# More weight buffers, low-half products last, deferred transposes and a moved modulation in a hybrid attention and FFN layer

## The chip, the core and the metric

The kernel runs on one core of a Trainium2 chip. TensorE (PE in the profile) multiplies, VectorE (DVE) and ScalarE (ACT) work elementwise, GpSimd (POOL) does a few additions and starts small transfers, and SyncE (SP) starts nearly all loads. The metric is the device time of one execution in microseconds (us); lower is better.

## The reference

One layer of a diffusion backbone over 256 latent tokens and 256 context tokens of width 2048, in float32. The parts that matter here:

```python
mod_x = split(silu(c) @ w_mod + b_mod, 6)         # shift1, scale1, gate1, shift2, scale2, gate2
h = rms_norm(x, g_mix) * (1 + scale1) + shift1    # the context with its own shift and scale
q, k, v, qb, kb, vb, rb, lr, ga, gb = split(h @ w_in)
o_attn = windowed_attention(rope(norm(q)), rope(norm(k)), v, context keys, sink)
o_gla = gated linear attention in two directions, started from the context
y = sigmoid(ga) * (o_attn @ w_attn_o) + sigmoid(gb) * ((norm(o_gla) * silu(rb)) @ w_gla_o)
x = x + gate1 * (y @ w_out)
u = conv3(modulate(x, g_ffn, shift2, scale2) @ w_up)   # 2 x 5632 columns
x = x + gate2 * ((silu(u_a) * u_g) @ w_down)
```

Every weight matrix is read from memory once; there are about 400 MB of them.

## The kernel before

**Exact products from halves.** PE multiplies float32 numbers that are cut into a high half `hi` and a low half `lo = x - hi`, and a product is the sum of three: high by high, high by low, low by high. `wsplit` (line 143) loads a half chunk of weights, two blocks of 128 rows by 512 columns, 512 KB, into a raw buffer, and cuts it: ACT copies it to `whi` (line 61), DVE subtracts to `wlo` (line 62). There are four raw buffers (`wr`, line 38) and three pairs of half buffers (`wh`, line 39).

**Two kinds of projection.** `proj_nat` (line 152) makes tokens by features: for each half chunk and each tile of 128 tokens, the activations are the stationary operand and the weights stream in 512 columns; lines 163 to 165 are the three products. `proj_T` (line 169) makes features by tokens: the weights are stationary and 256 tokens stream; lines 186, 188 and 189 are the three. Sums collect in four PSUM banks (`acc`); a projection with two token tiles takes two, one over latent and context tokens takes four. After its last half chunk, `evac` takes the banks out.

**Work beside the projections.** `tick` (line 124) runs once ahead of each half chunk. It advances a generator in `beside` (the linear attention `gla_A`, or the windowed attention `attend`) at a pace, and takes steps of a list `bg_steps` at the rate `bg_rate`. That list holds the later modulation: `mod_latent` (line 225) reads `w_mod` in 512 KB steps through the same raw buffers, and DVE multiplies each by a column of silu(c) and adds up in `macc` (line 239, two operations a step). After eight steps DVE transposes and reduces, and PE sums across partitions in the small product `pcl` (line 247). Parts 3, 4, 2 and 5 (shift2, scale2, gate1, gate2) are four times eight steps each.

**Stages in order.** Start: x and the context are transposed, shift1 and scale1 are made on PE, and with each group of rows of h that part of QB (two projections), KB and VB is added up (`add_to`, line 363). Then linear attention per head beside the next head's KB or VB block; the keys KA and values VA; four query blocks QA and one GA block with the windowed attention beside them; four RB blocks; the merge, which for each quarter of the columns runs GA, the attention's output matrix, GB and the linear attention's output matrix; the output projection; and the FFN, whose up projection is cut in a half of six blocks and one of five, each followed by its part of the down projection.

**Transposes at the end of a projection.** Token-major results that are needed feature-major are transposed on PE inside `evac`: `ptk` (line 680) and `ptq` (line 696) behind `norm_rope`, `to_T` (line 777, tile `pto`) in the RB blocks and the merge, and `ptx` (line 846) in the output projection. `rows_from_cols` (line 257) spreads a gate over all partitions: a transpose on PE, a copy, and two transfers by POOL by way of memory. gate1 is made ahead of the output projection, gate2 ahead of the up projection.

**What orders the instructions.** The program's order gives each instruction a rank, and a planner with its own idea of durations lays out each engine's stream ahead of the run: at each point the engine takes the highest ranked instruction that the planner takes to be ready. The split in `wsplit` has a raised rank. On the chip each engine works off its stream in order and waits where an input is late.

## Time and profile before

| | |
|---|---|
| median of three runs (us) | 2060.81 (2058.01 to 2062.3) |
| span of the profiled execution (us) | 2061.8 |
| mean granted PE clock | 0.990 |
| read from memory | 409.63 MB, 200 GB/s over the span |
| PE, DVE, ACT busy | 97%, 68%, 45% |

The profiled execution is told of by its span alone; it lies 1.0 us above the median of the runs. A row of groups reads: line, engine, operation, tile written <- tiles read, shapes, count | busy us, mean ns | idle time before and what ended it. A row of waits reads: who waited <- for whom: total us, times, longest. "SPq" is the queue of loads. Busy matmuls overlap, since a product starts before the one ahead of it has ended; the pace of PE is read from the distance of starts.

### The profile page before, as it was taken

To read this page: it belongs to the slowest core of one execution; us is meant where nothing else is said; L and a number is where in the kernel's file an instruction comes from. 1 tells how busy PE (TensorE), PEld (TensorE's weight loads), DVE (VectorE), ACT (ScalarE), POOL (GpSimd) and SP (SyncE) were. 2 spreads that over 40 slices of the span, in tenths; PEclk is the share of its full clock that TensorE was granted. 3 is DMA by queue.
4 is the path that set the end of the run, shared out by engine and by line. 5 is a ranking of instruction groups with operands and counts; after the bars stand their busy time and mean duration, and the time that the engine had idled before them with its cause. 6 is when DMAs were issued, how large, how long until landed. Compare 5 with 4: busy or idle time off the path is not lost.

```text
span 2061.8 us, 30115 instructions
## 1 busy us (share of the span) xinstructions
PE 1999.2 (97%) x11792; PEld 1721.8 (84%) x11792; DVE 1405.7 (68%) x2149; ACT 937.4 (45%) x1306; POOL 41.9 (2%) x62
## 2 busy tenths in 40 slices
PE   6899999999999999999999999899999999999999
PEld 4679888888787777777787788899999889999987
DVE  4666778978867888777767665666666555666654
ACT  3323464552346665443334344554455334445533
POOL 0001100001000000000000000000000000000000
PEclk8999999999999999999999999999999999999999
DMA  9976434347664466787888875566666566666664
GB/s 347 337 247 197 120 111 123 113 118 226 213 186 114 121 194 192 254 270 260 264 279 272 294 235 184 164 184 184 184 183 184 194 193 187 184 184 183 183 209 150
DMA packets 214350, 413.71 MB, mean 201 GB/s; under 512 B 12548, under 2 KB 21092, under 8 KB 213184
## 3 DMA queue, kind: packets, MB, share of 16 engines
q1 hardware_dynamic: 212320, 406.89, 63.3%
q0 software_dynamic: 1360, 4.74, 0.8%
q8 instruction: 92, 1.51, 0.3%
q14 instruction: 50, 0.41, 0.1%
q10 hardware_dynamic: 528, 0.17, 0.0%
HBM read 409.63 MB, written 2.11 MB: 200 GB/s over the span
## 4 chain that ended last, share of the span: by engine, by line
PE 60%; issue 18%; DMA 11%; DVE 8%; ACT 2%; POOL 0%; DVEq 0%; ACTq 0%; POOLq 0%
PE acc L189 10%; PE acc L186 10%; PE acc L188 10%; PE acc L165 8%; PE acc L164 8%; PE acc L163 8%; DMA raw<-in_w_mod 8%; DVE wlo L62 3%; DVE macc L239 2%; DMA raw<-in_w_in 2%; PE pm L210 1%; PE pa L503 1%; ACT whi L61 1%; DMA raw<-in_w_gla_o 1%; PE po L589 1%
## 5 line engine op out<-in xcount | busy, mean ns | idle before, releaser
L61 ACT ACTIVATE whi<-raw 128x1024 fp32r<-128x1024 f32 x568 | 601.4, 1059 | 863.7 <-PE acc L165 366.4
L62 DVE TENSOR_TENSOR wlo<-raw,whi 128x1024 fp32r<-128x1024 f32 x568 | 693.3, 1222 | 428.3 <-ACT whi L61 422.7
L186 PE MATMUL acc<-h2h,whi 128*128 128x256 f32 x1408 | 399.5, 284 | 1.3 <-ACT h2h L346 1.3
L188 PE MATMUL acc<-h2l,whi 128*128 128x256 f32 x1408 | 399.5, 284 | 0.0
L189 PE MATMUL acc<-h2h,wlo 128*128 128x256 f32 x1408 | 399.2, 284 | 0.0
L186 PEld LDWEIGHTS acc<-h2h,whi 128*128 128x128 f32 x1408 | 271.3, 193 | 1.9 <-ACT h2h L346 1.8
L188 PEld LDWEIGHTS acc<-h2l,whi 128*128 128x128 f32 x1408 | 271.3, 193 | 0.2
L189 PEld LDWEIGHTS acc<-h2h,wlo 128*128 128x128 f32 x1408 | 271.3, 193 | 0.0
L239 DVE SCALAR_TENSOR_TENSOR macc<-raw,ccol,macc 128x512 f32<-128x512 f32 x240 | 180.6, 752 | 100.5 <-DMA raw<-in_w_mod 97.2
L163 PE MATMUL acc<-whi,h01hi 128*128 128x512 f32 x352 | 139.5, 396 | 0.9 <-ACT whi L61 0.9
L164 PE MATMUL acc<-wlo,h01hi 128*128 128x512 f32 x352 | 139.1, 395 | 1.3 <-DVE wlo L62 1.2
L163 PE MATMUL acc<-whi,h00hi 128*128 128x512 f32 x352 | 139.2, 395 | 0.0
L164 PE MATMUL acc<-wlo,h00hi 128*128 128x512 f32 x352 | 139.0, 395 | 0.2 <-DVE wlo L62 0.2
L165 PE MATMUL acc<-whi,h00lo 128*128 128x512 f32 x352 | 138.6, 394 | 0.0
L165 PE MATMUL acc<-whi,h01lo 128*128 128x512 f32 x352 | 138.2, 392 | 0.0
L163 PE MATMUL acc<-whi,ah 128*128 128x512 f32 x352 | 137.0, 389 | 0.0
L164 PE MATMUL acc<-wlo,ah 128*128 128x512 f32 x352 | 137.0, 389 | 0.0
L165 PE MATMUL acc<-whi,al 128*128 128x512 f32 x352 | 136.9, 389 | 0.0
L164 PEld LDWEIGHTS acc<-wlo,h01hi 128*128 128x128 f32 x352 | 66.4, 189 | 16.0 <-DVE wlo L62 3.2
L163 PEld LDWEIGHTS acc<-whi,h01hi 128*128 128x128 f32 x352 | 66.4, 189 | 14.3 <-ACT whi L61 1.3
L164 PEld LDWEIGHTS acc<-wlo,h00hi 128*128 128x128 f32 x352 | 66.2, 188 | 14.1 <-DVE wlo L62 1.3
L165 PEld LDWEIGHTS acc<-whi,al 128*128 128x128 f32 x352 | 66.1, 188 | 13.8
(369 smaller groups left out, 3393.2 us busy)
## 6 DMA issues: line engine op xcount, KB each, us to landing
raw<-in_w_in SPq DMA_DIRECT2D x208, 512.0 KB, 4.2
raw<-in_w_up SPq DMA_DIRECT2D x176, 512.0 KB, 3.7
raw<-in_w_mod SPq DMA_DIRECT2D x128, 512.0 KB, 3.9
raw<-in_w_down SPq DMA_DIRECT2D x88, 512.0 KB, 3.8
mraw<-in_w_mod SPq DMA_DIRECT2D x32, 1024.0 KB, 10.2
raw<-in_w_attn_o SPq DMA_DIRECT2D x32, 512.0 KB, 4.8
raw<-in_w_gla_o SPq DMA_DIRECT2D x32, 512.0 KB, 5.2
raw<-in_w_out SPq DMA_DIRECT2D x32, 512.0 KB, 3.8
```

Source lines behind the costliest of these rows:

```text
L61: S.activation(hi, src, AF.Copy)
L62: V.tensor_tensor(lo, src, hi.bitcast(F32), op=ALU.subtract)
L163: PE.matmul(banks[i], ahi, hi[:, k, :], start=(kt == kts[0]), stop=False)
L164: PE.matmul(banks[i], ahi, lo[:, k, :], start=False, stop=False)
L165: PE.matmul(banks[i], alo, hi[:, k, :], start=False, stop=(kt == kts[-1]))
L186: PE.matmul(o, whi, ahi, start=(kt == kts[0] and b == 0), stop=False, skip_group_check=True)
L188: PE.matmul(o, whi, alo, start=False, stop=False, skip_group_check=True)
L189: PE.matmul(o, wlo, ahi, start=False, stop=(kt == kts[-1]), skip_group_check=True)
L210: PE.matmul(a[0][q:q + 32, :], cS[:, kt, :], raw[:, k, :], start=(kt < 4), stop=(kt >= 12))
L239: V.scalar_tensor_tensor(a[0], raw[:, k, :], ccol[:, kt:kt + 1], a[0], op0=ALU.mult, op1=ALU.add)
L503: PE.matmul(pa[:, t, :], k2[:, dt, t * P:(t + 1) * P], q2[:, dt, tq * P:(tq + 1) * P], start=(dt == 0), stop=(dt == 1))
L589: PE.matmul(po, x_, y_[:, s, :], start=(n == 0), stop=(n == 11))
```

## The change

- The raw buffers go from four to five, the pairs of half buffers from three to four. Room for them comes from the descriptor space of GpSimd's transfers (`dynamic_dma_scratch_size=4096`); the parameter rows of `columns` move to another pool.
- In both kinds of projection the products with the weights' low half are issued after all products with the high half of that half chunk.
- `defer(n, fn)` puts a piece of an evacuation on a list; `tick` counts down and runs it ahead of the half chunk that comes n + 1 ticks later. The transposes of KA, QA, RB, the merge and the output projection go there, and the last product of `mod_latent`. `flush` runs what is left.
- The steps of part 5 (gate2) leave the list that runs up to the merge and run beside the first half of the up projection, at 0.36 a half chunk; gate2 is spread over the partitions after it. The rates of the other steps change: 0.7 to 0.3, 2.0 to 1.6, 0.5 to 0.52.
- The windowed attention runs at 1.4 steps a half chunk instead of 0.8, starting at -2.9, so from the third half chunk on.

Removed comments aside, the diff is:

```diff
--- before.py
+++ after.py
@@ -35,8 +35,8 @@
...
     big = pool(name="big", bufs=16)
-    wr = pool(name="wr", bufs=4)
-    wh = pool(name="wh", bufs=3)
+    wr = pool(name="wr", bufs=5)
+    wh = pool(name="wh", bufs=4)
     f2 = pool(name="f2", bufs=1)
...
@@ -100,7 +100,7 @@
...
     def columns(name, parts, eng=G):
-        rows = W2("mod", "rows", [P, P])
+        rows = sm.tile([P, P], F32, name="rows", tag="t128", bufs=2)
         n = 0
...
@@ -115,14 +115,27 @@
...
     beside = []
+    later = []
+    def defer(n, fn):
+        later.append([n, fn])
+    def flush():
+        while later:
+            later.pop(0)[1]()
...
+        for e in later:
+            e[0] -= 1
+        while later and later[0][0] < 0:
+            later.pop(0)[1]()
         if beside:
...
@@ -161,13 +174,16 @@
...
                     PE.matmul(banks[i], ahi, hi[:, k, :], start=(kt == kts[0]), stop=False)
-                    PE.matmul(banks[i], ahi, lo[:, k, :], start=False, stop=False)
-                    PE.matmul(banks[i], alo, hi[:, k, :], start=False, stop=(kt == kts[-1]))
+                    PE.matmul(banks[i], alo, hi[:, k, :], start=False, stop=False)
+            for i, l in enumerate(lhs):
+                for k in range(nk):
+                    kt = k0 + k
+                    PE.matmul(banks[i], l(kt)[0], lo[:, k, :], start=False, stop=(kt == kts[-1]))
         for i in range(len(lhs)):
...
@@ -175,26 +191,27 @@
...
             hi, lo = wsplit(w[k0 * P:(k0 + nk) * P, c0:c0 + 512])
-            for f in range(4):
-                for k in range(nk):
-                    kt = k0 + k
-                    whi, wlo = (x[:, k, f * P:(f + 1) * P] for x in (hi, lo))
-                    for i, r in enumerate(rhs):
-                        b = (f % per) if n == 1 else i
-                        o = banks[f // per][:, b * T:(b + 1) * T]
-                        ahi, alo = r(kt)
-                        PE.matmul(o, whi, ahi, start=(kt == kts[0] and b == 0), stop=False,
-                                  skip_group_check=True)
-                        PE.matmul(o, whi, alo, start=False, stop=False, skip_group_check=True)
-                        PE.matmul(o, wlo, ahi, start=False, stop=(kt == kts[-1]), skip_group_check=True)
+            for part in range(2):
+                for f in range(4):
+                    for k in range(nk):
+                        kt = k0 + k
+                        w_ = (lo if part else hi)[:, k, f * P:(f + 1) * P]
+                        for i, r in enumerate(rhs):
+                            b = (f % per) if n == 1 else i
+                            o = banks[f // per][:, b * T:(b + 1) * T]
+                            ahi, alo = r(kt)
+                            PE.matmul(o, w_, ahi, start=(kt == kts[0] and b == 0 and part == 0),
+                                      stop=(kt == kts[-1] and part == 1), skip_group_check=True)
+                            if part == 0:
+                                PE.matmul(o, w_, alo, start=False, stop=False, skip_group_check=True)
         for i in range(len(banks)):
...
@@ -243,19 +260,23 @@
...
                 V.tensor_reduce(rs, tr, op=ALU.add, axis=AX.X)
-                pc = bank("pcl", (32, 16))
-                PE.matmul(pc, sel[:, 0:32], rs, start=True, stop=True)
-                pv = pc.rearrange("p (a b) -> p b a", b=4)
-                d = dst[:, 4 * j:4 * j + 4]
-                for b4 in range(4):
-                    V.tensor_copy(d[32 * b4:32 * b4 + 32, :], pv[:, b4, :])
-                b0 = part * 16 + j * 4
-                V.tensor_tensor(d, d, bmod[:, b0:b0 + 4], op=ALU.add)
+                def out():
+                    pc = bank("pcl", (32, 16))
+                    PE.matmul(pc, sel[:, 0:32], rs, start=True, stop=True)
+                    pv = pc.rearrange("p (a b) -> p b a", b=4)
+                    d = dst[:, 4 * j:4 * j + 4]
+                    for b4 in range(4):
+                        V.tensor_copy(d[32 * b4:32 * b4 + 32, :], pv[:, b4, :])
+                    b0 = part * 16 + j * 4
+                    V.tensor_tensor(d, d, bmod[:, b0:b0 + 4], op=ALU.add)
+                defer(3, out)
...
@@ -597,11 +618,11 @@
...
-    for part, dst in ((3, shift2), (4, scale2), (2, gcol1), (5, gcol2)):
+    for part, dst in ((3, shift2), (4, scale2), (2, gcol1)):
         for j in range(4):
             bg_steps.extend(mod_latent(part, j, dst))
-    bg_rate[:] = [0.7, 0.0]
+    bg_rate[:] = [0.3, 0.0]
...
@@ -675,12 +696,16 @@
...
         z = norm_rope(b, rk if i < 2 else None, i % 2)
-        pt = bank("ptk", (P, 4, P))
-        for h in range(4):
-            PE.transpose(pt[:, h, :], z[:, h, :], ident)
-        split(kTh[:, :, i * P:(i + 1) * P], kTl[:, :, i * P:(i + 1) * P], pt)
-    bg_rate[0] = 2.0
+        def turn():
+            pt = bank("ptk", (P, 4, P))
+            for h in range(4):
+                PE.transpose(pt[:, h, :], z[:, h, :], ident)
+            split(kTh[:, :, i * P:(i + 1) * P], kTl[:, :, i * P:(i + 1) * P], pt)
+        defer(1 + i // 2, turn)
+    bg_rate[0] = 1.6
     proj_nat(w_in, 0, KA, ALL, h_xc, ka_evac)
...
@@ -691,10 +716,14 @@
...
             z = norm_rope(b, rq, t)
-            pt = bank("ptq", (P, 4, P))
-            for h in range(4):
-                PE.transpose(pt[:, h, :], z[:, h, :], ident)
-            split(qT[:, 0, :, t * P:(t + 1) * P], qT[:, 1, :, t * P:(t + 1) * P], pt)
+            def turn():
+                pt = bank("ptq", (P, 4, P))
+                for h in range(4):
+                    PE.transpose(pt[:, h, :], z[:, h, :], ident)
+                split(qT[:, 0, :, t * P:(t + 1) * P], qT[:, 1, :, t * P:(t + 1) * P], pt)
+            defer(2 + t, turn)
...
@@ -759,14 +788,14 @@
...
     for g in range(4):
-        beside[:] = [attend(g, qTs), 0.8, 0.0]
+        beside[:] = [attend(g, qTs), 1.4, -2.9]
         qTs = qa_block(g + 1) if g < 3 else ga_block()
...
-    bg_rate[0] = 0.5
+    bg_rate[0] = 0.52
     glan = W2("fb", "glan", [P, 512])
...
@@ -787,7 +816,7 @@
...
             V.tensor_tensor(s_, s_, o_, op=ALU.mult)
-            to_T(s_, gh, gl, j, t)
+            defer(1 + t, lambda: to_T(s_, gh, gl, j, t))
...
@@ -818,16 +847,15 @@
...
             V.tensor_tensor(a2[t], a2[t], a1[t], op=ALU.add)
-            to_T(a2[t], mh, ml, j, t)
+            defer(1 + t, lambda: to_T(a2[t], mh, ml, j, t))
...
-    while bg_steps:
-        bg_steps.pop(0)()
+    assert not bg_steps
     x1 = [M(f"x1_{t}", [P, D]) for t in range(2)]
...
@@ -841,15 +869,20 @@
...
             S.activation(y, x1[t][:, js], AF.Square, accum_out=ss1[:, t, j:j + 1])
-            pt = bank("ptx1", (P, 4, P), side=True)
-            for k in range(4):
-                PE.transpose(pt[:, k, :], x1[t][:, j * 512 + k * P:j * 512 + (k + 1) * P], ident)
-            dst = x1T[j // 2][:, (j % 2) * 4:(j % 2) * 4 + 4, t * P:(t + 1) * P]
-            S.activation(dst, pt, AF.Copy)
+            def turn():
+                pt = bank("ptx1", (P, 4, P), side=True)
+                for k in range(4):
+                    PE.transpose(pt[:, k, :], x1[t][:, j * 512 + k * P:j * 512 + (k + 1) * P], ident)
+                dst = x1T[j // 2][:, (j % 2) * 4:(j % 2) * 4 + 4, t * P:(t + 1) * P]
+                S.activation(dst, pt, AF.Copy)
+            defer(1 + t, turn)
...
+    flush()
     s1 = sm.tile([P, 2], F32, name="s1", bufs=1)
...
@@ -861,7 +894,9 @@
...
                      scale2[:, kt:kt + 1], shift2[:, kt:kt + 1])
-    gate2 = rows_from_cols("gate2", gcol2)
+    for j in range(4):
+        bg_steps.extend(mod_latent(5, j, gcol2))
+    bg_rate[:] = [0.36, 0.0]
     h2 = [lambda kt: (h2h[kt // 8][:, kt % 8, :], h2l[kt // 8][:, kt % 8, :])]
...
@@ -891,8 +926,12 @@
...
             proj_T(w_up, DFF + j * 512, ALL, h2, lambda p_, b: up_evac(p_, b, 1))
+        if half == 0:
+            assert not bg_steps
+            flush()
+            gate2 = rows_from_cols("gate2", gcol2)
         for j in range(4):
-            def dn_evac(t, b, j=j, half=half):
+            def dn_evac(t, b, j=j, half=half, gate2=gate2):
                 js = slice(j * 512, (j + 1) * 512)
...
@@ -941,7 +980,8 @@
...
-    nc = bacc.Bacc("TRN2", target_bir_lowering=False, num_devices=1)
+    nc = bacc.Bacc("TRN2", target_bir_lowering=False, num_devices=1,
+                   dynamic_dma_scratch_size=4096)
     arrays, aps = {}, {}
...
```

## The prediction

> **What bounds the kernel now.** I read the page first: its first two parts say which engine fills the span and at what clock.
>
> ```profile
> PE 1999.2 (97%) x11792; PEld 1721.8 (84%) x11792; DVE 1405.7 (68%) x2149; ACT 937.4 (45%) x1306; POOL 41.9 (2%) x62
> ```
>
> PE is busy for 1999.2 of 2061.8 us, so at most 62.6 us of idle PE time, and what it loses to a lower clock, can be won without removing work; the change removes none. The next view, busy time in chosen stretches (start:end and length, then PE, PEld, DVE, ACT and POOL, clock, DMA share, GB/s), shows where the idle time lies.
>
> ```profile
> 0.00:100.00 100.00, 75.11 (x546) 55.02 (x547) 52.61 (x125) 36.27 (x58) 2.98 (x9) 0.90 0.97 340
> 250.00:500.00 250.00, 244.73 (x1314) 209.59 (x1313) 209.50 (x400) 132.38 (x269) 24.42 (x31) 1.00 0.44 130
> 600.00:795.00 195.00, 194.17 (x908) 152.34 (x908) 165.79 (x347) 117.55 (x209) 0.00 (x0) 1.00 0.52 151
> 795.00:865.00 70.00, 65.96 (x300) 52.96 (x299) 57.89 (x79) 31.95 (x39) 0.58 (x1) 0.98 0.75 237
> 865.00:1212.00 347.00, 335.15 (x1472) 268.66 (x1471) 250.21 (x314) 139.30 (x142) 0.00 (x0) 1.00 0.82 270
> 1303.00:1314.00 11.00, 7.46 (x35) 6.75 (x35) 7.09 (x22) 4.57 (x13) 1.06 (x2) 0.53 0.41 141
> 1314.00:1606.00 292.00, 292.00 (x2361) 288.74 (x2361) 186.01 (x240) 148.94 (x185) 0.00 (x0) 1.00 0.63 182
> ```
>
> The start loses 24.9 us beside DMA engines at a share of 0.97; linear attention 5.3; the windowed attention 0.8; the RB blocks 4.0; the merge 11.85; the head of the FFN 3.5 at a clock of 0.53. From 1314 us PE never idles in the first up projection: nothing can be won there, only lost. Third view: what PE waited for (total, times, longest).
>
> ```profile
> PE pto L779 <- DVE m L820: 5.0, 3, 2.2
> PE acc L164 <- DVE wlo L62: 5.0, 9, 2.0
> PE acc L189 <- DVE wlo L62: 4.7, 7, 1.2
> PE ptk L680 <- DVE sq L671: 4.4, 1, 4.4
> PE pa L568 <- DVE kf L561: 3.2, 4, 1.0
> PE pto L779 <- DVE sr L789: 3.1, 3, 1.9
> PE pa L503 <- DVE q L523: 2.3, 4, 0.9
> PE acc L163 <- ACT whi L61: 0.9, 1, 0.9
> PE pcl L247 <- DVE mrs L245: 0.9, 1, 0.9
> PE pto L779 <- DVE scale L856: 0.8, 1, 0.8
> ```
>
> Two families: transposes placed in the stream ahead of their DVE input (pto, ptk, pcl), and products with the low half of a weight that wait for its subtraction on DVE (wlo).
>
> **Part 1: deferred transposes.** The later place is behind one to four half chunks, each 12 products in a token projection. Their spacing is in the timeline (start, duration, engine and line):
>
> ```profile
> 1230.63 0.39 PE L163 MATMUL acc<-whi,mh 128*128 128x512 f32 x1
> 1230.85 0.39 PE L164 MATMUL acc<-wlo,mh 128*128 128x512 f32 x1
> 1231.08 0.39 PE L165 MATMUL acc<-whi,ml 128*128 128x512 f32 x1
> ```
>
> Some 0.225 us each; I use 0.227, so 2.7 us a half chunk, above the longest of the pto waits (2.2). The key block has 24 products a half chunk, 5.4 us, above 4.4. All of these waits should go: 5.0 + 3.1 + 0.8 = 8.9 for pto and 4.4 for ptk. The transposes themselves and the copies behind them are only moved. After an idle stretch PE also runs slow for a while:
>
> ```profile
> 540.52 1.11 PE L680 MATMUL ptk<-ident,sq 128*128 128x128 f32 x4 [4.36 <-DVE sq L671]
> 542.28 0.63 PE L165 MATMUL acc<-whi,h10lo 128*128 128x512 f32 x1
> 542.71 0.63 PE L163 MATMUL acc<-whi,h10hi 128*128 128x512 f32 x1
> 859.23 0.95 PE L779 MATMUL pto<-ident,sr 128*128 128x128 f32 x4 [1.93 <-DVE sr L789]
> 538.50:545.30 6.80, 4.78 (x14) 3.91 (x15) 5.24 (x14) 2.77 (x4) 0.00 (x0) 0.50 0.41 126
> 859.40:862.80 3.40, 3.40 (x11) 2.82 (x10) 3.33 (x6) 0.60 (x1) 0.00 (x0) 0.50 0.78 258
> ```
>
> Behind the first wait the spacing is 0.43 instead of 0.227, at a clock of 0.50. Of that stretch some 4 us lie behind the wait, of the second, at 0.50 too, about 3; each loses nearly half: 1.9 and 1.4. So ptk is worth 6.3 and pto 10.3. The Trainium skill, "TensorE: Matmul & The Clock Gate", section "The HAM clock gate", puts the drop to half rate behind an idle window of about 3.4 us; by that rule only the 4.36 us wait would pay it and the sum would be 1.4 us smaller. The trace differs: a wait of 1.93 us was followed by a clock of 0.50 too, and the measurement decides.
>
> **Part 2: low halves last, four half buffers, five raw buffers.** The count of products and weight loads stays (x11792 each), and the spacing does not depend on whether a stationary operand repeats: in the three rows above mh stands twice, then ml, 0.22 and 0.23 apart, and in the up projection wlo, then whi twice, 0.13 and 0.11 apart:
>
> ```profile
> 1400.46 0.28 PE L189 MATMUL acc<-h2h,wlo 128*128 128x256 f32 x1
> 1400.59 0.28 PE L186 MATMUL acc<-h2h,whi 128*128 128x256 f32 x1
> 1400.70 0.28 PE L188 MATMUL acc<-h2l,whi 128*128 128x256 f32 x1
> ```
>
> So the new order costs nothing by itself. Its worth is time: the first low product stands 8 products (1.8 us) into a token half chunk instead of 1, and 16 (1.9 us) into an up half chunk instead of 2. In the merge all named waits, 5.0 + 0.9 + 0.9 beside the pto's 5.0, make up the 11.85. Their cause, from the waits and groups of that stretch (865 to 1212 us), the DMA issues of the page and, last, the waits of the up projection (1340 to 1600 us) for comparison:
>
> ```profile
> DVE macc L239 <- DMA raw<-in_w_mod: 60.3, 37, 3.4
> SPq L68 <- DVE wlo L62: 177.7, 119, 4.4
> L239 DVE SCALAR_TENSOR_TENSOR macc<-raw,ccol,macc 128x512 f32<-128x512 f32 x104 | 77.9, 749 | 61.7 <-DMA raw<-in_w_mod 60.3
> raw<-in_w_gla_o SPq DMA_DIRECT2D x32, 512.0 KB, 5.2
> ACT whi L61 <- PE acc L188: 109.7, 76, 1.9
> ```
>
> SP issues a load only when one of four raw buffers comes free: it waited 119 times for a subtraction to free one, 177.7 us in all, and a modulation load in its order holds up the weight load behind it. DVE works in order too, and stands 60.3 us before a modulation load that has not landed, with a subtraction queued behind, and PE behind that. Some 119 weight loads and 104 / 2 = 52 modulation loads in 347 us are 0.49 a us; four buffers then turn in 8.1 us, of which the landing takes up to 5.2. Five, at the same 8.1, carry 0.62, and the fourth half buffer lets the splits run a half chunk further ahead. I take 5.3 of the 6.8, as the rows name a cause for all of it but a late load can still outlast the lead; bounds 0 and 6.8. At the start, 4.7 us of wlo waits lie where DMA is at 0.97, and PE set free would wait for loads: I take 1.0, bounds 0 and 4.7.
>
> A cost comes with the order: banks finish together. Before, the first of two banks had its last product 6 products before the end; now 2. The head of the FFN and the kernel's end wait for that chain on DVE (two 0.68 us operations a tile), so each gets 4 x 0.227 = 0.9 later: +1.8. With four banks, the first finished 18 products (4.1 us) ahead and now 6 (1.4 us). Where the next projection needs those banks at once (KB to VB and VB to the next QB in five groups, KA to VA, VA to QA: 12 places), a bank's evacuation (0.69) must not stand behind a split:
>
> ```profile
> L62 DVE TENSOR_TENSOR wlo<-raw,whi 128x1024 fp32r<-128x1024 f32 x21 | 25.4, 1219 | 4.9 <-ACT whi L61 4.8
> L363 DVE TENSOR_TENSOR qb<-qb,acc 128x512 f32<-128x512 f32 x12 | 8.2, 686 | 13.7 <-PE acc L189 13.6
> ```
>
> 1.4 holds 0.69 alone, not 0.69 + 1.22. Bounds 0 and 12 x 1.22 = 14.6; between 100 and 200 us, where these rows are from, DVE waits for PE (13.6 us), so mostly it is free: 0.2 each, +2.4.
>
> **Part 3: modulation moved.** 32 of the 128 steps go from before the FFN into the up projection's first six blocks: 96 half chunks x 0.36 = 34.6, enough for 32. The others now take 0.3 x 32 + 1.6 x 16 = 35.2 steps before the attention and 60.8 / 0.52 = 117 half chunks of the 152 after it. In linear attention DVE loses four of seven steps:
>
> ```profile
> L239 DVE SCALAR_TENSOR_TENSOR macc<-raw,ccol,macc 128x512 f32<-128x512 f32 x54 | 41.2, 763 | 13.9 <-DMA raw<-in_w_mod 13.3
> ```
>
> 41.2 x 4/7 = 23.5 us less on a DVE that is busy for 209.5 of 250. The waits of pa (3.2 + 2.3) are the ends of long DVE chains; I take 1.5 of 5.5, bounds 0 and 5.5. In the up projection (six blocks, 2304 products at 0.12 us, about 276 us) each step adds two operations of 0.75: 48 us, and DVE goes from 186/292 = 64% to some 81%; a load more per 2.8 half chunks raises 182 GB/s to about 248, below the merge's 270. With five raw buffers the need is 1.36 loads in 2.87 us, 0.47 a us, against the 0.62 above. Products wait if DVE stands before a modulation load for longer than the lead. Nearest row: the whole merge loses 11.85 us beside 52 steps, 0.23 a step, or 7.3 for 32. That is the upper bound; as half of those were transposes, and lead and buffers are larger: +1.0, lower bound 0 (PE has no idle time to gain).
>
> The gate rows now begin only after the up projection, and the first evacuation that reads them stands behind 24 x 2 x 3 = 144 products at 0.227, 32.7 us:
>
> ```profile
> gate<-dgate POOLq DMA_DIRECT2D x2, 1024.0 KB, 6.6
> dgate<-row POOLq DMA_DIRECT2D x2, 8.0 KB, 1.9
> ```
>
> Copies included some 10 us: hidden, 0; without that cover it would be 10. The attention's pace changes with equal work; PE idles only 0.8 of the 195 us there: 0, bounds -0.8 and +3 (a pto-like wait or two more). The smaller descriptor space touches POOL's few transfers, 41.9 us of issue off every chain: 0; if a broadcast were cut in pieces, twice 6.6 for the gates, still inside 32.7. Rows in another pool: 0, since POOL's loads of them end long before use.
>
> **Sum.** -6.3 - 10.3 - 5.3 - 1.0 - 1.5 + 1.8 + 2.4 + 1.0 = -19.2, from 2061.8 to 2042.6. The profiled execution lies 1.0 above the median, so 2041.6.
>
> **The rivals.** *Load-bound merge*: the fifth buffer changes little, as DMA stays at 0.82 and DVE still stops at each late load; only the transposes pay: without 5.3, 1.0 and 1.5, 2049. For it: the 60.3 us. *More gain*: also the start's 4.7 and all of pa's 5.5 and of the merge's 6.8: 9.2 more, 2032. Against it: DMA at 0.97. *Banks late*: each of 12 places waits a whole split, 12.2 more: 2054. *Slower: modulation starves the up projection.* Each step holds DVE for a late load, beyond the lead, and PE, which has no idle time there, stops. It decides from 23.3 / 32 = 0.73 us a step over my value of 0.03; at the merge's mean late load (60.3 in 37 waits, 1.6 us) 32 steps cost 51: 2092. Against it: ACT, which splits first, waits there for PE (109.7 us), not for loads, so a lead is there to be used, and the demand is under the merge's. *No effect*: the planner that orders the instructions puts the transposes where they were and the low products still wait: 2060.8 and, with some of the costs of 5.2, about 2063.
>
> **How the numbers follow.** Forecast 0.48; more gain 0.18; load-bound merge 0.13; banks late 0.08; no effect 0.05; slower 0.08. A measurement tells some 0.2% (4.1 us) from no change, so faster is below 2056.7: the first four, less a share of the banks' case, 0.85; same, to 2064.9: 0.06; slower 0.09. The range takes in more gain with the lower costs at nothing (2032 less 5) and the late banks: 2027 to 2056; that leaves out the slow rival, no effect and a little of the rest, under 0.2.
>
> **What would show it.** PE's waits without ptk and pto and no clock of 0.50 near 540 and 860 us; wlo waits of the merge below 2 us; idle PE of the merge under 3 of 11.85; up projection still at 100% of PE with DVE near 81%; the head about 0.9 longer. Wrong would be: PE waiting for wlo beside macc after 1300 us, first products of VB or VA waiting for an evacuation, or merge time that moved less than its waits.

## The result, and the profile after

The changed kernel takes 2068.92 us (median of 13 runs, 2064.26 to 2073.52), against 2060.81 of the kernel before on the same chip: a ratio of 1.0035, 95% interval 1.0023 to 1.0046. It is 0.35% slower where 0.9% faster was forecast. The profiled execution took 2069.64 us, with a span of 2067.9, 6.1 more than before.

The page's first part, of the changed kernel:

```profile
PE 1997.5 (97%) x11792; PEld 1725.3 (83%) x11792; DVE 1400.1 (68%) x2149; ACT 937.6 (45%) x1309; POOL 42.4 (2%) x62
```

The work is the same, to the product. Busy time in the same stretches as before (start:end and length, then PE, PEld, DVE, ACT and POOL, clock, DMA share, GB/s):

```profile
0.00:100.00 100.00, 77.75 (x586) 57.95 (x590) 54.39 (x129) 37.94 (x61) 2.99 (x9) 0.93 1.00 352
250.00:500.00 250.00, 241.95 (x1288) 206.48 (x1287) 193.40 (x364) 132.09 (x269) 24.39 (x31) 1.00 0.36 107
600.00:795.00 195.00, 190.96 (x884) 149.60 (x883) 159.71 (x324) 115.31 (x199) 0.00 (x0) 1.00 0.53 157
865.00:1212.00 347.00, 335.86 (x1481) 275.03 (x1480) 231.52 (x279) 141.29 (x145) 0.52 (x1) 0.99 0.77 253
1303.00:1314.00 11.00, 5.05 (x21) 4.02 (x21) 7.12 (x21) 4.79 (x14) 0.00 (x0) 0.52 0.39 124
```

The start gained (PE 75.1 to 77.8). Linear attention lost though DVE does less there (209.5 to 193.4 us). The merge still idles for 11.1 of 347 us, after 11.85. The waits of PE (total, times, longest) say why:

```profile
PE pto L808 <- DVE m L849: 9.8, 4, 5.8
PE pr L317 <- DVE dg L316: 9.7, 3, 3.7
PE pa L524 <- DVE q L544: 5.1, 4, 2.0
PE ptk L703 <- DVE sq L692: 5.0, 1, 5.0
PE pa L589 <- DVE kf L582: 4.2, 4, 1.3
PE acc L181 <- DVE wlo L62: 1.3, 2, 0.9
PE pto L808 <- DVE sr L818: 1.0, 1, 1.0
```

The low halves are on time (wlo 5.0 to 1.3 in the merge). But the transposes that were deferred so as not to wait still wait: pto for 10.8 us (8.9 before), ptk for 5.0 (4.4).

Both kernels issue the same 10,272 products of projections, so each stage's end can be compared by the start of its last one. Lead over the kernel before, in us (negative is ahead); each column is one profiled execution, so a few us of any entry can be that execution's own. Two kernels below show how much: the changed one and the same with a later start of the moved modulation issue the same instructions in the same order up to 1289 us, and still lie 4.4 us apart at the end of the output projection.

| end of | after | mixed | order alone | later slots | old order in linear attention | old order RB to merge |
|---|---|---|---|---|---|---|
| start | -3.4 | -5.1 | -4.8 | -4.6 | -3.6 | -4.4 |
| KA | +3.0 | -4.3 | +2.1 | +1.9 | -2.1 | +2.8 |
| RB blocks | +8.8 | -1.5 | +5.4 | +5.9 | +0.3 | +7.9 |
| output projection | +1.2 | -17.8 | +9.3 | -8.5 | -6.0 | -6.7 |
| first up projection | +5.2 | -13.9 | +9.6 | -4.7 | -2.2 | -4.4 |
| last product | +5.3 | -13.8 | +9.6 | -4.6 | -2.0 | -4.2 |

The changed kernel loses 6.4 us in linear attention and KA, 5.8 up to the RB blocks, gains only 7.6 in merge and output projection, and loses 4.0 at the FFN's head and in its up projection. The other columns are experiments below.

Where the merge's gain went is seen at the end of its second quarter. DVE's timeline in the kernel before (start, duration, lines; in brackets the idle time ahead and what ended it), whose bank's last product ended at 1020.24:

```profile
1017.41 1.54 DVE L239 SCALAR_TENSOR_TENSOR macc<-raw,ccol,macc 128x512 f32<-128x512 f32 x2 [1.60 <-DMA raw<-in_w_mod]
1018.87 1.22 DVE L62 TENSOR_TENSOR wlo<-raw,whi 128x1024 fp32r<-128x1024 f32 x1
1020.44 1.22 DVE L62 TENSOR_TENSOR wlo<-raw,whi 128x1024 fp32r<-128x1024 f32 x1 [0.34 <-ACT whi L61]
1021.58 1.28 DVE L819 TENSOR_TENSOR m<-acc,m 128x512 f32<-128x512 f32 x2
```

and in the changed kernel, first DVE, then PE around the same place:

```profile
1023.71 1.54 DVE L256 SCALAR_TENSOR_TENSOR macc<-raw,ccol,macc 128x512 f32<-128x512 f32 x2 [1.62 <-DMA raw<-in_w_mod]
1025.16 2.35 DVE L62 TENSOR_TENSOR wlo<-raw,whi 128x1024 fp32r<-128x1024 f32 x2
1029.77 1.54 DVE L256 SCALAR_TENSOR_TENSOR macc<-raw,ccol,macc 128x512 f32<-128x512 f32 x2 [2.25 <-DMA raw<-in_w_mod]
1031.22 0.68 DVE L848 TENSOR_TENSOR m<-acc,m 128x512 f32<-128x512 f32 x1
1031.82 1.22 DVE L62 TENSOR_TENSOR wlo<-raw,whi 128x1024 fp32r<-128x1024 f32 x1
1032.95 0.68 DVE L849 TENSOR_TENSOR m<-m,m 128x512 f32<-128x512 f32 x1
```

```profile
1021.01 1.21 PE L181 MATMUL acc<-wlo,gh 128*128 128x512 f32 x4 [0.87 <-DVE wlo L62]
1026.62 1.08 PE L181 MATMUL acc<-wlo,h00hi 128*128 128x512 f32 x4
1027.63 0.23 PE L266 MATMUL pcl<-mrs,sel 128*32 128x16 f32 x2
1033.69 1.12 PE L808 MATMUL pto<-ident,m 128*128 128x128 f32 x4 [5.83 <-DVE m L849]
```

Before, one split stood between the bank's end and the evacuation, which began 1.3 us behind it. Now two splits and two modulation pairs (a pair is the two `macc` operations of one step) stand there, both pairs late for their loads, and a third split stands between the evacuation's two operations. The bank was full at 1022.22; its evacuation began at 1031.22, 9.0 us later, and the tile was ready at 1033.64. PE came for it 5.6 us behind the bank's end, later than before (1.8) but not late enough.

### The profile page after: what moved, and what is told of

The parts are those of the page before. It is cut to its first block, busy times and chain, and to the rows that moved or that the text cites. A ratio compares the mean times of both kernels' runs of the same rounds, so it can differ in the third digit from the quotient of the medians.

```text
span 2067.9 us, 30113 instructions
## 1 busy us (share of the span) xinstructions
PE 1997.5 (97%) x11792; PEld 1725.3 (83%) x11792; DVE 1400.1 (68%) x2149; ACT 937.6 (45%) x1309; POOL 42.4 (2%) x62
## 4 chain that ended last, share of the span: by engine, by line
PE 65%; issue 20%; DMA 7%; DVE 7%; ACT 1%; POOL 0%; DVEq 0%; ACTq 0%; POOLq 0%; SPq 0%
PE acc L203 20%; PE acc L176 10%; PE acc L177 10%; PE acc L181 10%; PE acc L206 10%; DMA raw<-in_w_mod 6%; DVE macc L256 2%; DVE wlo L62 2%; PE pm L227 2%; PE pa L524 1%; PE pa L589 1%; PE po L610 1%; PE plr L454 0%; ACT whi L61 0%; PE pto L808 0%
## 5 line engine op out<-in xcount | busy, mean ns | idle before, releaser
L203 PE MATMUL acc<-h2h,whi 128*128 128x256 f32 x1408 | 347.2, 284 | 1.5 <-ACT h2h L367 1.5
L206 PE MATMUL acc<-h2l,whi 128*128 128x256 f32 x1408 | 346.8, 284 | 0.0
L256 DVE SCALAR_TENSOR_TENSOR macc<-raw,ccol,macc 128x512 f32<-128x512 f32 x240 | 180.7, 753 | 137.0 <-DMA raw<-in_w_mod 133.9
L203 PE MATMUL acc<-h2h,wlo 128*128 128x256 f32 x1408 | 198.4, 284 | 0.0
L203 PEld LDWEIGHTS acc<-h2h,wlo 128*128 128x128 f32 x1408 | 182.4, 193 | 0.0
L181 PE MATMUL acc<-wlo,h01hi 128*128 128x512 f32 x352 | 98.0, 393 | 0.0
L181 PE MATMUL acc<-wlo,h00hi 128*128 128x512 f32 x352 | 97.4, 393 | 0.0
L181 PE MATMUL acc<-wlo,ah 128*128 128x512 f32 x352 | 94.1, 389 | 0.0
L176 PEld LDWEIGHTS acc<-whi,h00hi 128*128 128x128 f32 x352 | 67.0, 190 | 15.6 <-ACT kb L382 0.7
L181 PEld LDWEIGHTS acc<-wlo,h00hi 128*128 128x128 f32 x352 | 66.3, 189 | 13.8
L181 PEld LDWEIGHTS acc<-wlo,ah 128*128 128x128 f32 x352 | 66.1, 188 | 13.7
```

What stands on the lines that cost most here:

```text
L176: PE.matmul(banks[i], ahi, hi[:, k, :], start=(kt == kts[0]), stop=False)
L181: PE.matmul(banks[i], l(kt)[0], lo[:, k, :], start=False, stop=(kt == kts[-1]))
L203: PE.matmul(o, w_, ahi, start=(kt == kts[0] and b == 0 and part == 0), stop=(kt == kts[-1] and part == 1), skip_group_check=True)
L206: PE.matmul(o, w_, alo, start=False, stop=False, skip_group_check=True)
L256: V.scalar_tensor_tensor(a[0], raw[:, k, :], ccol[:, kt:kt + 1], a[0], op0=ALU.mult, op1=ALU.add)
```

## The experiments

All ratios are to the kernel before, run beside each kernel, with a 95% interval.

### Each part taken out

Modulation of the second gate back ahead of the FFN:

```diff
-    for part, dst in ((3, shift2), (4, scale2), (2, gcol1)):
+    for part, dst in ((3, shift2), (4, scale2), (2, gcol1), (5, gcol2)):
...
-    bg_rate[:] = [0.3, 0.0]
+    bg_rate[:] = [0.7, 0.0]
...
-    bg_rate[0] = 1.6
+    bg_rate[0] = 2.0
...
-    bg_rate[0] = 0.52
+    bg_rate[0] = 0.5
...
-    bg_rate[:] = [0.36, 0.0]
+    gate2 = rows_from_cols("gate2", gcol2)
```

> The changed kernel with the modulation of gate2 put back ahead of the FFN at the old rates (0.7, 2.0, 0.5); buffers, order and deferral stay. Theory A (the moved steps stand in the FFN's head: in the trace of the changed kernel two products of macc, waiting for their load, lie between the steps of the root in the head, which grew from 9.3 to 12.3 us): the head shrinks back and the kernel gains some 4 us on the changed one, about 2064; the earlier stages get their old load back. Theory B (the new order of products or the deeper buffers cost): no more than 1 us away from the changed kernel, about 2068, the head included. My sum before had the move at -0.5, so by it 2069.

Measured: 1.0034 (1.0021 to 1.0048), as slow as the change. The second: the old numbers of buffers.

```diff
-    wr = pool(name="wr", bufs=5)
-    wh = pool(name="wh", bufs=4)
+    wr = pool(name="wr", bufs=4)
+    wh = pool(name="wh", bufs=3)
```

> The changed kernel with four raw buffers and three pairs of halves. Theory A (the fifth raw buffer serves the weights alone, since a modulation load is issued the moment a modulation product has freed a buffer and turns once in some 5.6 us in both kernels): waits for low halves in the merge return in part, +2 to +4, about 2071, and DVE's wait for modulation loads stays within 10 us of what it is. Theory B (the deeper lookahead puts splits ahead of other DVE work, which is why the waits of pa, pto and ptk are longer): these waits shrink and the kernel gains 5 us or more, 2063 or less.

Measured: 1.0011 (1.0001 to 1.0022): the two more buffers cost about 0.24% here. The third: the old order of products in both kinds of projection (the lines with a minus in the diff above put back).

> The changed kernel with the old order of the three products. Theory A (the order costs only the late banks at the two ends, 1.8 us, and wins the low halves' waits in the merge, some 4 us): slower by 2 to 3, about 2071. Theory B (evacuations that begin up to 2.7 us later push the chains behind them past their deferred places): pto, pa and ptk waits shrink by 5 us or more together, about 2063.

Measured: 1.0016 (1.0006 to 1.0027). Its profile holds two opposite effects: 11.1 us ahead at the end of the output projection, 7.5 behind at the end of the up projection (its profiled execution lies 5.4 us above its median, so the second is large rather than exact). The fourth: `defer` runs its function at once.

```diff
     def defer(n, fn):
-        later.append([n, fn])
+        fn()
```

> The changed kernel with every deferred piece run at once, so that the transposes have their old rank. Theory A (a deferred transpose still waits when the DVE work ahead of it stands behind a modulation product whose load is late; deferral helps where DVE is only slow): pto and ptk waits grow from 16 us to 20 or more, about 2073. Theory B (deferral only moves the waits): the same sum of pto, ptk and ptx waits within 2 us, about 2068.

Measured: 1.0022 (1.0013 to 1.0032). Without the deferral the changed kernel is, if anything, faster: the deferral gains nothing in it. PE waited for pto in the merge for 6.4 and 7.1 us in two quarters, with DVE's evacuation 6.2 and 7.3 us late, so DVE is late without the deferral too.

### The order alone, and the order mixed

The kernel before with the new order in both kinds of projection, the token projections (`proj_nat`) and the feature projections (`proj_T`), and nothing else:

> The kernel before with the new order of products in both kinds of projection and nothing else of the change. Theory (the token order spoils the evacuations): the transposes stand where they stood, behind a bank that ends with its neighbour and behind a DVE order with a split between the two operations; PE's waits for pto rise from 9.0 us to 13 or more (14.1 in the version without deferral), those for wlo fall below 2 us, and the time is 3 to 10 us longer than before, 2064 to 2072. Rival (the order is harmless by itself, only its meeting with the new pace and the moved modulation costs): wlo falls, pto stays near 9, and the time is 2 to 5 us shorter.

Measured: 1.0065 (1.0041 to 1.0089), 13 us. Its waits of PE:

```profile
PE pto L783 <- DVE m L824: 13.6, 3, 5.7
PE pto L783 <- DVE sr L793: 3.2, 2, 2.4
```

The wlo waits are gone and pto waits for 16.8 us instead of 8.9: the order that was costed at nothing, but for some turnarounds, costs more by itself than the whole change does (1.0035). Then the mixed kernel: everything of the change, but the token projections keep the old order.

```diff
     def proj_nat(w, r0, c0, kts, lhs, evac):
...
-                    PE.matmul(banks[i], alo, hi[:, k, :], start=False, stop=False)
-            for i, l in enumerate(lhs):
-                for k in range(nk):
-                    kt = k0 + k
-                    PE.matmul(banks[i], l(kt)[0], lo[:, k, :], start=False, stop=(kt == kts[-1]))
+                    PE.matmul(banks[i], ahi, lo[:, k, :], start=False, stop=False)
+                    PE.matmul(banks[i], alo, hi[:, k, :], start=False, stop=(kt == kts[-1]))
```

> The changed kernel with the old order of products in the token projections alone (low half second, as before); the up projections keep the low halves last. Theory A (the order costs in token projections, where it moves the end of the first bank and so its evacuation behind a modulation product in DVE's order, and pays in the up projection under the moved modulation): it combines the 11 us lead that the kernel with the old order everywhere has at the end of the output projection with an up projection without waits; idle PE at pto about 2 us; about 7 us faster than before, 2056. Theory B (any edit reshuffles the planner's streams and the leads are luck of one layout): lead at the end of the output projection anywhere between 6 behind and 2 ahead, total within 4 us of the changed kernel.

Measured: 2051.28 us, 0.9942 (0.9929 to 0.9954): faster than both kernels. Its DVE at the end of the second quarter, where the bank was full at 1009.52:

```profile
1009.38 1.54 DVE L253 SCALAR_TENSOR_TENSOR macc<-raw,ccol,macc 128x512 f32<-128x512 f32 x2 [1.59 <-DMA raw<-in_w_mod]
1010.84 2.35 DVE L62 TENSOR_TENSOR wlo<-raw,whi 128x1024 fp32r<-128x1024 f32 x2
1013.11 1.28 DVE L845 TENSOR_TENSOR m<-acc,m 128x512 f32<-128x512 f32 x2
```

One modulation pair fewer stands ahead and no split between: the first tile is ready 5.5 us behind the bank's end and PE comes at 5.6, so it waits for nothing there, by a hair; for the second tile it waits 1.0 us.

### Order or slot

Precedence in planning for the evacuations of the token projections, in the changed kernel:

```diff
-        for i in range(len(lhs)):
-            evac(i, banks[i])
+        with tc.high_priority():
+            for i in range(len(lhs)):
+                evac(i, banks[i])
```

> The changed kernel with the evacuations of the token projections given precedence in the planning of the instructions; products, deferral and modulation as in the change. Theory (the loss lies in DVE's planned order, a split and a modulation step ahead of the evacuation, and not in the products): pto falls from 10.9 us to 4 or less and the time to 2050 to 2057. Rival (both banks end together and DVE is late whatever its order): pto stays at 8 or more and the time at 2064 to 2070.

Measured: 1.0046 (1.0029 to 1.0063). The edit didn't do what it was meant to: DVE's order at the merge's evacuations stayed as in the change, a split between the two operations included, so the run says nothing on the order. Later slots do: the same order on DVE at those places, with the transposes of the RB blocks and the merge three half chunks later.

```diff
-            defer(1 + t, lambda: to_T(s_, gh, gl, j, t))
+            defer(4 + t, lambda: to_T(s_, gh, gl, j, t))
...
-            defer(1 + t, lambda: to_T(a2[t], mh, ml, j, t))
+            defer(4 + t, lambda: to_T(a2[t], mh, ml, j, t))
```

> The changed kernel with the transposes of the RB blocks and of the merge deferred by three more half chunks (4 and 5 instead of 1 and 2, some 11 us behind the bank's end); DVE's order of work stays that of the change. Theory (the slot is too early, as DVE gets the tile ready 9.4 to 11.4 us after the bank's end): pto falls from 10.9 us to 2 or less, the half clock behind it goes too, 2055 to 2062. Rival (DVE itself is behind by then, and PE only waits for the next split instead): pto falls, wlo waits of 5 us or more take its place, 2065 to 2070.

Measured: 1.0001 (0.9991 to 1.0011), some 7 us better than the change by the ratios. PE's waits for pto fell from 10.8 to 0.6 us; in the merge none is left, only 4.4 us in eight waits for wlo.

The old token order put back in one place each, by a switch in `proj_nat`, off in linear attention in the first kernel, off from the RB blocks to the merge's end in the second:

```diff
+    low_last[0] = False
     a, kb1 = with_gla(0, kbt, kb_block)
...
+    low_last[0] = True
     att = M("att", [P, 2048])
```

```diff
     bg_rate[0] = 0.52
+    low_last[0] = False
...
+    low_last[0] = True
     assert not bg_steps
```

> The changed kernel with the old order of products in the token projections beside linear attention alone. Theory (the new token order costs the 6.4 us that the changed kernel loses between the start and the key block): that stretch loses 2 us or less, pa falls from 9.9 us to 7.5 or less, and the time is 2062 to 2066. Rival (the pace of the modulation or the buffers cost it): the stretch still loses 5 us or more, 2067 to 2071.

> The changed kernel with the old order of products in the token projections of the RB blocks, the merge and the output projection alone. Theory (the new token order pushes a modulation pair ahead of the evacuation): the first evacuation of the merge begins 2 to 4.5 us behind the bank's end instead of 7 to 9, pto is 2 us or less, and the time is 2056 to 2062. Rival (the lead of the mixed kernel comes from elsewhere): the time stays at 2065 to 2070. If this and the run on linear attention hold all that the mixed kernel gained, their gains add up to about 17.

The output projection kept the new order in this kernel, unlike what the text above says. Measured: 1.0002 (0.9992 to 1.0012) and 1.0009 (0.9999 to 1.0018), so 0.33% and 0.26% better than the change; together about 12 us of the 19 that the mixed kernel gains on it. In the second, the evacuations of the merge's first two quarters began 4.1 and 3.6 us behind the bank's end, not 7.0 and 9.0. In linear attention and KA (217 to 530 us) the busy time of the kernel before, and of the kernel with the old order in linear attention:

```profile
217.00:530.00 313.00, 307.52 (x1775) 262.06 (x1774) 255.55 (x469) 158.10 (x308) 29.58 (x37) 1.00 0.48 143
```

```profile
217.00:530.00 313.00, 305.74 (x1753) 259.49 (x1752) 233.00 (x426) 158.89 (x309) 26.95 (x36) 1.00 0.40 120
```

The changed kernel's PE is busy for 302.88 us of the same stretch. The new token order thus costs linear attention about 3 us of busy PE in that window, and by the table 4.9 by the end of KA. Where the rest of the 19 us lies was not tried: the start, KA, VA, the query blocks and the output projection kept the new order in both runs.

Of the waits and evacuations at the ends of the merge's first two quarters, from the timelines (us behind the bank's last product):

| kernel | evacuation begins | first tile ready | PE comes | PE waits for it |
|---|---|---|---|---|
| before | 2.3, 1.3 | 4.2, 3.2 | 2.1, 1.8 | 2.2, 1.5 |
| order alone | 4.0, 5.9 | 6.4, 8.4 | 2.7, 2.7 | 3.8, 5.7 |
| after | 7.0, 9.0 | 9.4, 11.4 | 8.3, 5.6 | 1.1, 5.8 |
| after, old buffers | 5.8, 7.3 | 8.2, 9.7 | 8.9, 7.2 | 0, 2.5 |
| after, later slots | 4.7, 9.3 | 7.1, 11.8 | 11.1, 12.3 | 0, 0 |
| after, old order RB to merge | 4.1, 3.6 | 5.9, 5.5 | 8.7, 5.6 | 0, 0 |
| mixed | 2.1, 3.6 | 3.9, 5.5 | 8.3, 5.6 | 0, 0 |
| deferral and buffers (below) | 4.0, 4.5 | 5.9, 6.3 | 2.7, 2.7 | 3.2, 3.7 |

With the deferral, PE comes 2.7 us behind the bank where the transposes stand first in the list of deferred work, and later where a modulation's last product (pcl), deferred by three, stands ahead of them: the list is worked from its front. The row pcl right ahead of the wait for pto above is such a place.

### Why the mixed kernel gains

Four kernels have the old token order, the deferral and the buffers, with and without the move of the modulation and the new order in the feature projections; their edits are those shown above, put together. Neither:

> The changed kernel with the old order of products in both kinds of projection and the second gate's modulation back ahead of the FFN at the old rates: the deferral, the buffers and the attention's pace are left. Theory (the deferral is what gains, and the new order in the up projection pays only because the modulation was put there): PE idles for nothing in the first up projection, pto stays below 2 us, and the time is that of the mixed kernel within 4 us, 2047 to 2055. Rival (the new order in the feature projections has a worth of its own, at the start and in linear attention): wlo waits of 4 us or more return outside the up projection and the time is 2056 to 2062.

Measured: 0.9997 (0.9986 to 1.0008). The new feature order alone, without the move:

> The mixed kernel (old order in the token projections, new order in the feature projections, deferral, buffers) with the second gate's modulation back ahead of the FFN at the old rates. Theory (the move empties DVE in the merge, and the new feature order only pays for it in the up projection): the merge's evacuations stand behind a finished modulation part and a split as in the kernel with deferral alone, pto is 8 us or more, and the time is 2054 to 2062. Rival (the new feature order is the gain, the move is neutral): pto is below 3 us and the time is 2047 to 2053.

Measured: 0.9991 (0.9981 to 1.0001). The move alone is the kernel with the old order in both (1.0016), and both is the mixed kernel (0.9942): each is worth nothing or less by itself, and together they gain. At the end of the merge's first quarter, with neither, DVE and PE show

```profile
925.74 1.54 DVE L252 SCALAR_TENSOR_TENSOR macc<-raw,ccol,macc 128x512 f32<-128x512 f32 x2 [1.64 <-DMA raw<-in_w_mod]
927.20 1.22 DVE L62 TENSOR_TENSOR wlo<-raw,whi 128x1024 fp32r<-128x1024 f32 x1
928.33 0.64 DVE L266 COPY gcol<-pcl 32x4 f32<-32x4 f32 x4
929.09 1.23 DVE L62 TENSOR_TENSOR wlo<-raw,whi 128x1024 fp32r<-128x1024 f32 x1
930.23 1.28 DVE L844 TENSOR_TENSOR m<-acc,m 128x512 f32<-128x512 f32 x2
```

```profile
932.17 0.98 PE L804 MATMUL pto<-ident,m 128*128 128x128 f32 x4 [3.24 <-DVE m L845]
```

Here it is the end of a part of the modulation that stands ahead of the evacuation, at each of the first three quarters. At 0.5 steps a half chunk a quarter of 32 half chunks holds two whole parts of eight steps, so the kernel with the new feature order and without the move was also run at a rate of 0.52:

```diff
-    bg_rate[0] = 0.5
+    bg_rate[0] = 0.52
```

> The fourth corner (old token order, new feature order, modulation not moved) at a rate of 0.52 instead of 0.5 steps a half chunk from the RB blocks on. Theory (the phase: at 0.5 each quarter of the merge ends where a part of the modulation is finished, whose product has left the list, so the transposes come 2.7 us behind the bank and wait): at 0.52 the wait is 3 us or less in all and the time is 2050 to 2055. Rival (the number of steps: DVE works through 32 more of them up to the FFN, and is late whatever their phase): pto stays at 6 us or more and the time at 2055 to 2061.

Measured: 1.0024 (1.0013 to 1.0035); pto waits 12.6 us. At the ends of the first three quarters the evacuation is 5.3, 1.5 and 4.9 us late: a modulation pair stands ahead of it in the first and third, only a split in the second. The run doesn't settle whether it is the phase, since at 0.52 too no modulation product stood ahead of the transposes in the list and PE came 2.7 to 3.0 us behind the bank.

What the move gives in the merge is two things. The modulation ends within the third quarter, so that quarter's evacuation begins as the bank fills (0.4 us ahead of the modelled end of its last product) instead of 3.1 us late; the fourth begins so in every kernel above. And at the ends of the first two quarters of each kernel with the move and the deferral a modulation's last product stands ahead of the transposes, so that PE comes at 8.3 and 5.6 us in the mixed kernel, against 2.7 in the kernel with the new feature order and no move. In the second quarter the evacuation is 3.6 us late in both of these, and only PE's arrival differs: 2.8 us of wait against none. That slot was chosen by nobody; it falls out of the pace of the modulation, and is luck as much as design. How much of the gain it is was not tried.

What the move takes is seen in the up projection with the old order everywhere (1308 to 1620 us):

```profile
DVE macc L252 <- DMA raw<-in_w_mod: 62.1, 22, 5.6
PE acc L202 <- DVE wlo L62: 10.2, 11, 2.0
```

where the changed kernel shows no wlo wait at all behind the head. There the new order does what it was costed for: the low half is due 16 products into a half chunk instead of 2, and DVE's stops before modulation loads (30.5 us there) don't reach PE.

### Other sizes and costs

The mixed kernel with four raw and three half buffers, and with the keys' transposes (ptk) two half chunks later:

```diff
-        defer(1 + i // 2, turn)
+        defer(3 + i // 2, turn)
```

> The mixed kernel (old order in the token projections, new order in the feature projections) with four raw and three half buffers as before. Theory (the two more buffers only let the splits run ahead of the evacuations): the time falls by 2 to 5 us below the mixed kernel, 2046 to 2049, as it did by 4.7 under the new order. Rival (with the old token order the buffers shelter the products): wlo waits rise from 2.8 us to 6 or more and the time rises by 3 to 6 us, 2054 to 2057.

> The mixed kernel (old order in the token projections, new order in the feature projections) with the transposes of the attention's keys deferred by two more half chunks of 24 products, 10.9 us more. Theory (the slot is too early there too: the keys are ready 11.9 us behind the last product, PE comes after 7.0): ptk falls from 4.8 us to 1 or less and the time to 2044 to 2049. Rival (the keys' chain on DVE is pushed back as far, or the next block's transposes wait for the same banks): a wait of 3 us or more stays or turns up behind it, 2050 to 2054.

Measured for the first: 0.996 (0.9949 to 0.9971), the same as the mixed kernel or a little slower: with the old token order the two more buffers don't cost, and without them PE waits for wlo for 11.4 us instead of 2.8. For the second: 0.9962 (0.995 to 0.9974): ptk is gone, but

```profile
PE acc L176 <- ACT y L674: 4.7, 1, 4.7
```

The first products of a later block now wait for a bank that ACT has not yet emptied, which they don't in the mixed kernel. The wait only changed its name.

The moved modulation starting later, in the mixed kernel and in the changed one:

```diff
-    bg_rate[:] = [0.36, 0.0]
+    bg_rate[:] = [0.36, -2.0]
```

> The kernel of the mixed order, and the moved modulation starting in the ninth half chunk of the up projection instead of the third (phase -2.0, same rate). Theory A (two modulation products are planned into the FFN's head and hold the root's small steps): the head, from the last product of the output projection to the first of the up projection, is back at 9 us and the total 3 us under the mixed order's. Theory B (the head's length is set by the transposes of the last block): unchanged within 1 us.

> The changed kernel with only the later start of the moved modulation (phase -2.0). The stages ahead of the FFN are unchanged in the program, so their times should stand; the head falls from 12 to some 9 us: 3 us faster than the changed kernel by the theory of the head. If the head is due to the later end of the banks and the deferral, less than 1 us.

Measured: 0.9941 (0.9928 to 0.9953) and 1.0027 (1.0014 to 1.004), each as without it. At the FFN's head of the changed kernel DVE shows

```profile
1306.52 0.75 DVE L256 SCALAR_TENSOR_TENSOR macc<-raw,ccol,macc 128x512 f32<-128x512 f32 x1 [1.32 <-DMA raw<-in_w_mod]
1307.19 0.15 DVE L305 TENSOR_TENSOR newt<-rstd 128x2 f32<-128x2 f32 x1
```

a modulation pair inside the Newton step (its second operation follows at 1307.31). With the later start the head is shorter (from the last product of the output projection to the first of the up projection 10.1 us instead of 11.35, and 8.9 instead of 12.35 in the mixed kernel), but the first up projection is longer (285.4 us instead of 280.65, 282.1 instead of 279.65) and takes most of it back, or more.

Three raw buffers for weights and two for the modulation, in the changed kernel:

```diff
-    def wload(src):
+    def wload(src, tag="raw"):
...
-        raw = wr.tile([P, 2, 512], F32, name="raw", tag="raw")
+        raw = wr.tile([P, 2, 512], F32, name=tag, tag=tag, bufs=3 if tag == "raw" else 2)
...
-            raw = wload(w_mod[k0 * P:k0 * P + 256, c0:c0 + 512])
+            raw = wload(w_mod[k0 * P:k0 * P + 256, c0:c0 + 512], "rawm")
```

> The changed kernel with the five raw buffers divided: three for weights, two for the modulation alone. Theory A (modulation loads turn on the one buffer that a modulation product has just freed, so DVE, in order, stands before nearly each of them with evacuations queued behind): with a second buffer each load is issued one step ahead, DVE's wait for modulation loads falls from 134 us to under 50, and pto's 10.9 to under 4: 8 us or more faster than the changed kernel. Theory B (the transposes wait for DVE's own work): DVE's wait for loads falls, pto stays within 3 us.

Measured: 1.0205 (1.019 to 1.022). The start is 49.5 us behind; that its weights now turn on three buffers is the likely reason, not a tried one. PE's waits for the start's own modulation loads and for pto are

```profile
PE pm L227 <- DMA mraw<-in_w_mod: 26.7, 6, 12.7
PE pto L808 <- DVE m L849: 9.7, 3, 5.1
```

DVE's wait for the modulation loads in `macc` fell from 133.9 to 78.2 us, not to under 50, and pto didn't move. The price of the start hides what the own buffers are worth in time.

## Why the prediction was wrong, step by step

**The step that failed: part 1's "all of these waits should go".** It set the deferral of 2.7 us against the longest pto wait of 2.2, as if PE had come for the transposes as the bank filled, and as if DVE's evacuation stayed where it was on the clock. Neither held. PE already came 2.1 and 1.8 us behind the bank's end in the kernel before, so a slot at 2.7 (the row of deferral and buffers) is only 0.6 and 0.9 us later, and tiles ready at 4.2 and 3.2 us, as they were before, would still have been late for it. And with the change the evacuation moved from 2.3 and 1.3 us behind the bank's end to 7.0 and 9.0. With the modulation's product ahead of the transposes, PE's arrival moved by 6.2 and 3.8 us, and the tile's readiness by 5.2 and 8.2. So -10.3 for pto became about +2 in waits (8.9 to 10.8), with the half clock behind them: around the 5.83 us wait PE's clock is

```profile
1030.50:1040.70 10.20, 5.79 (x17) 4.62 (x18) 9.78 (x18) 2.35 (x4) 0.00 (x0) 0.50 0.75 227
```

where the sum took the half clock behind such waits as won. Later slots, the only edit in that run, took these waits away and gave back some 7 us: shown.

Forecast and measured span lie 25.3 us apart (2042.6 and 2067.9). The 16.6 us of both kinds of transposes that didn't come are the larger part; linear attention and KA, where 6.4 were lost and 1.5 forecast as won, are most of the rest, as far as terms can be set beside stages.

**Part 2's "the new order costs nothing by itself".** Right of the products' pace, wrong of the kernel: alone it costs 13 us. The forecast did see that banks end together, and put +1.8 and +2.4 on it at 12 turnarounds in the start and the attention and at two ends. The kernel's end got 0.7 us longer, near the 0.9 given. The large price was elsewhere, in linear attention and at evacuations that feed a transpose: at the ends of the merge's first two quarters the planner put a modulation pair more ahead of the evacuation, and a split between its two operations. The split there goes with the order of the products: it is in the runs with the new token order and not in those with the old. The pair isn't tied as firmly, as it also stands ahead with the old order in the run at 0.52. Why the planner chooses so was not looked into.

**Part 2's waits for wlo, -5.3 in the merge.** Right by the row: 5.0 to 1.3. It bought nothing, as the same DVE stopped PE at pto instead; idle PE in the merge went from 11.85 to 11.1, where under 3 was named as the sign.

**Part 2's rate of loads, 0.62 with five buffers.** Wrong for the modulation, which was the late one. The waits of the merge (865 to 1212 us) in the changed kernel:

```profile
DVE macc L256 <- DMA raw<-in_w_mod: 56.8, 32, 3.3
ACT whi L61 <- PE acc L177: 107.6, 68, 2.8
SPq L68 <- DVE wlo L62: 169.7, 118, 4.4
```

DVE stood for 56.8 us at 40 modulation loads, 60.3 at 54 before: 1.4 us a load instead of 1.1. The buffers went to weights: ACT, which splits first, now waits 107.6 us for PE to free a half buffer, 56.5 before. The loads of the sync engine (start, duration of the issue) show the reason:

```profile
1019.85 0.37 SPq L68 DMA_DIRECT2D raw<-in_w_mod  x1
1020.98 1.50 SPq L68 DMA_DIRECT2D raw<-in_w_in  x2
1025.27 0.37 SPq L68 DMA_DIRECT2D raw<-in_w_mod  x1
```

The load issued at 1025.27 begins 0.02 us after the modulation pair at 1023.71 has ended, and DVE takes it up at 1029.77, 4.5 us later: a modulation load starts as the pair of the load before it ends, so it turns on one buffer, as it did before (5.8 us from load to load in the median then, 5.6 now).

**ptk, -6.3.** Wrong for the same reason: the keys were ready 11.6 us behind the last product before and 13.6 after, while PE came at 7.3 and 8.6: a deferral credited with 5.4 us moved PE's arrival by 1.3. In the mixed kernel, deferring it enough cost the same elsewhere.

**Start, -1.0:** 3.4, inside its bounds of 0 and 4.7. **Linear attention, -1.5:** outside its bounds of 0 and 5.5 less: the waits of pa rose from 5.5 to 9.3 by the rows above (5.1 and 4.2). Four of seven steps did leave DVE, and the new token order took more than that gave.

**Part 3.** Right where it was thought riskiest: PE stayed at 100% in the up projection; DVE and DMA stand at

```profile
1314.00:1606.00 292.00, 292.00 (x2367) 288.95 (x2366) 227.15 (x330) 148.17 (x188) 1.06 (x2) 0.99 0.73 235
```

78% and 235 GB/s, forecast 81% and 248. Up projection and head cost 4.0 together (1.5 and 2.5) where 1.9 was given, mostly by the modulation pair in the head's Newton step, which was not thought of: with the modulation back ahead of the FFN, the head took 9.1 us, against 8.9 before and 11.35 after. The rival that ended slower put the loss here, at wlo behind macc; that is what the kernel with the old order in both shows, not the changed one. The 41.9 us that the prediction calls POOL's issue are its busy time; nothing hung on it.

## What to carry to other kernels

A deferred consumer waits as before if the engine that feeds it is filled in order by a planner: compare the time at which the input is ready behind its own trigger with the time at which the consumer comes, not the old wait with the new slack, since the consumer may already come late. Late loads that an in-order engine must pass belong away from the evacuations, and an order of products that suits one kind of projection should be tried on each kind by itself, since here its sign differs.

## What the runs showed of the hardware

A short stop of PE can cost clock too, but its length alone doesn't decide. In the changed kernel a wait of 1.84 us in linear attention (timeline of PE) is followed by 3.6 us at 0.53 (the busy time of two stretches behind it):

```profile
248.60 1.84 PE L524 MATMUL pa<-q,kb 128*128 128x128 f32 x8 [1.84 <-DVE q L544]
```

```profile
248.60:252.20 3.60, 3.60 (x18) 3.60 (x19) 2.76 (x7) 1.95 (x4) 0.00 (x0) 0.53 0.09 31
252.20:256.00 3.80, 3.80 (x34) 3.80 (x34) 3.35 (x6) 0.78 (x3) 0.00 (x0) 1.00 0.02 4
```

The Trainium skill, "TensorE: Matmul & The Clock Gate", section "The HAM clock gate", has full rate come back about 4 us into sustained products; the 3.6 us here agree with that. Its idle window of about 3.4 us ahead of the drop doesn't: 1.84 us were enough, as the 1.93 us in the kernel before. Yet the clock stayed at 1.00 behind a wait of 2.20 us in the kernel before (it ended at 928.87) and one of 2.03 us in the changed kernel (at 438.38), the busy time behind them in that order:

```profile
929.20:932.60 3.40, 3.40 (x19) 2.67 (x18) 3.40 (x5) 2.14 (x3) 0.00 (x0) 1.00 0.67 204
438.40:442.00 3.60, 3.60 (x20) 3.16 (x21) 3.42 (x9) 1.98 (x4) 0.00 (x0) 1.00 0.86 319
```

What makes the difference stays open.
